# Row sums of a 16384 x 1024 array: another assignment of rows to partitions, line-aligned buffers, and a last row in equal halves

## The chip, the cores and the metric

The kernel runs on one core of a Trainium2 chip. The metric is the device time in microseconds (us); three runs of the kernel before gave a median of 161.55 us.

## The reference

`x` has shape 32 x 512 x 1024 in float32, and the output is `np.sum(x, axis=-1)`, 32 x 512 in float32. Taken flat, there are 16,384 rows of 1,024 numbers (4 KB a row, 67.1 MB in all), and one sum is wanted for each row (64 KB in all).

## The kernel before

The 16,384 rows are spread over the 128 partitions of the on-chip memory, 128 rows for each. They are cut into 8 groups of 2,048 consecutive rows (`x_g`, L120). Within a group, partition p has the 16 rows from 16p on, one run of 64 KB in device memory; the next partition's run follows directly behind it. `rows_from(j, n)` (L123) gives the n rows from the j-th on of every partition. The sums of partition p stand in 128 columns of the tile `sums`, 16 to a group. `out_v` (L121) is the same division of the output, so that a group's sums are 16 consecutive numbers (64 B) for each partition.

Data goes into the tile `t`, of which there are three buffers ("in", bufs=3), each of 16 x 1024 + 4 words in a partition. Every load is issued by SyncE in the helper `rows` (L180). The order is:

1. the first 7 rows of the last group (FIRST = 7). This load is moved to the program's entry, ahead of the start-up barrier;
2. groups 0 to 6, each as one load of 16 rows for every partition (8 MB). From the third buffer on, SyncE may issue a load only when the reduction that read its buffer has ended. Two more waits (`hold`) keep the second load behind a small activation of ScalarE, and the third behind the first reduction;
3. the other 9 rows of the last group, all into one buffer: 6 rows, then 2 rows, then the last row in two pieces, columns 0 to 535 (L231) and 536 to 1023 (L232).

The arithmetic:

- VectorE sums the first 7 rows and groups 0 to 5 with one reduction for each load (`vec`, L141).
- From group 6 on the rows of a load are shared: VectorE takes a row at a time with an add of its two halves that also sums the result (`halves`, L155, each followed by an instruction that reads the sum out), ScalarE takes the others with an activation that accumulates (`act`, L168).
- The last row's first piece is summed to a word that stands right ahead of the second piece (so the second piece is written one word further on); a zero behind the second piece makes the number of words even (L229). The last add then covers that partial sum, the 488 columns and the zero, as two halves of 245 words.

ScalarE's queue stores the sums of groups 0 to 6 (`store`, L191, 7 x 16 columns for each partition), which must wait until the load of 2 rows has landed. SyncE stores the last group's 16 columns after the last add. A hook (`wait_for_the_store_at_the_clear`) has GpSimd wait for that last store at the end of the program.

The seed is one word that VectorE clears (L198) and the small activation reads (L200).

Of the kernel before, what the change touches and what calls it, by code (L numbers as in the profile page):

```python
# [100 lines left out]
@with_exitstack  # L101
def kernel(
    ctx: ExitStack,
    tc: tile.TileContext,
    x: bass.AP,
    out: bass.AP,
):
    nc = tc.nc
    nc.at_finalize(issue_first_load_at_entry)
    nc.at_finalize(order_waits)  # L110
    nc.at_finalize(wait_for_the_store_at_the_clear)
    fp32 = mybir.dt.float32
    P = 128
    batch, seq, dim = x.shape
    rows = batch * seq
    J = rows // P
    BIG = 16


    x_g = x.flatten_outer_dims().rearrange("(g p j) d -> g p j d", p=P, j=BIG)  # L120
    out_v = out.rearrange("b s -> (b s)").rearrange("(g p j) -> p g j", p=P, j=BIG)  # L121

    def rows_from(j, n):  # L123
        return x_g[j // BIG, :, j % BIG : j % BIG + n, :]

    last = J // BIG - 1
    FIRST = 7
    pieces = (536, 488)  # L130

    with (
        tc.tile_pool(name="in", bufs=3) as inpool,
        tc.tile_pool(name="unread", bufs=4, space=bass.MemoryType.PSUM) as upool,
        tc.tile_pool(name="stage", bufs=1) as stpool,
        tc.manual_schedule(),
    ):
        sums = stpool.tile([P, J], fp32)

        def vec(dst, src):  # L140
            return nc.vector.tensor_reduce(  # L141
                out=dst, in_=src, axis=mybir.AxisListType.X, op=mybir.AluOpType.add
            )

        def hold(inst, until, reason):
            tc.add_manual_dep(
                inst.ins,
                until.ins.name,
                mybir.DependencyInfo(mybir.DependencyClass.Sync, mybir.DependencyReason.DATA),
                reason=reason,  # L150
            )

        def halves(dst, src):
            n = src.shape[-1] // 2
            return nc.vector.tensor_tensor_reduce(  # L155
                out=src[:, :n],
                in0=src[:, :n],
                in1=src[:, n:],
                scale=1.0,
                scalar=0.0,  # L160
                op0=mybir.AluOpType.add,
                op1=mybir.AluOpType.add,
                accum_out=dst,
            )

        def act(dst, src, n):
            unread = upool.tile([P, dim], fp32)
            nc.scalar.activation(  # L168
                out=unread[:, :n],
                in_=src,  # L170
                func=mybir.ActivationFunctionType.Copy,
                accum_out=dst,
            )

        sums_of = []

        def rows(t, a, n, j, n_act, pairs=False):
            nv = n - n_act
            block = t[:, a * dim : (a + n) * dim].rearrange("p (n d) -> p n d", d=dim)
            load = nc.sync.dma_start(out=block, in_=rows_from(j, n))  # L180
            if pairs:
                for q in range(nv):
                    sums_of.append(halves(sums[:, j + q : j + q + 1], block[:, q, :]))
            else:
                sums_of.append(vec(sums[:, j : j + nv], block[:, :nv, :]))
            for q in range(nv, n):
                act(sums[:, j + q : j + q + 1], block[:, q, :], dim)
            return load

        def store(eng, g0, g1):  # L190
            return eng.dma_start(  # L191
                out=out_v[:, g0:g1],
                in_=sums[:, g0 * BIG : g1 * BIG].rearrange("p (g j) -> p g j", j=BIG),
            )


        seed = stpool.tile([P, 1], fp32)
        nc.vector.memset(seed, 0.0)  # L198
        unread = upool.tile([P, dim], fp32)
        ready = nc.scalar.activation(  # L200
            out=unread[:, :1], in_=seed, func=mybir.ActivationFunctionType.Copy
        )

        j = last * BIG
        t = inpool.tile([P, BIG * dim + 4], fp32)
        rows(t, 0, FIRST, j, 0)
        first = sums_of[-1]
        for g in range(last):
            t = inpool.tile([P, BIG * dim + 4], fp32)
            if g < last - 1:  # L210
                load = rows(t, 0, BIG, g * BIG, 0)
            else:
                rows(t, 0, BIG, g * BIG, 7, pairs=True)
            if g == 0:
                hold(load, ready, "no second load while the first one's descriptors are made")
            if g == 1:
                hold(load, first, "no descriptors of later loads while the first ones start")

        t = inpool.tile([P, BIG * dim + 4], fp32)
        rows(t, FIRST, 6, j + FIRST, 2, pairs=True)  # L220
        two = rows(t, FIRST + 6, 2, j + FIRST + 6, 1, pairs=True)
        a = BIG - 1

        j += a
        c, width = pieces
        whole = t[:, a * dim + c : BIG * dim + 2]
        nc.vector.memset(whole[:, width + 1 :], 0.0)  # L229
        part = t[:, a * dim : a * dim + c]  # L230
        nc.sync.dma_start(out=part, in_=rows_from(j, 1)[:, 0, :c])  # L231
        nc.sync.dma_start(out=whole[:, 1 : width + 1], in_=rows_from(j, 1)[:, 0, c:])  # L232
        hold(store(nc.scalar, 0, last), two, "its packets come behind those of the loads")
        halves(whole[:, :1], part)
        halves(sums[:, j : j + 1], whole)
        store(nc.sync, last, last + 1)


# [28 lines left out]
```

## Time and profile before

| what | value |
|---|---|
| median of three runs | 161.55 us (161.54 to 162.11) |
| span of the profiled execution | 159.83 us |
| median less that span | 1.72 us |
| VectorE busy | 120.7 us, 76% |
| ScalarE busy | 12.1 us, 8% |
| DMA packets | 2,784, 67.18 MB, mean 420 GB/s |
| reduction of 16 rows | 17.22 us, six times |
| reduction of 7 rows | 7.62 us, once |
| add of 512 words | 0.69 us, 14 times |
| activation of 1,024 words | 1.01 us, ten times |

The profiled execution's own time beside its span is not listed, only those of the three runs; so the table gives the distance from the span to their median. The span runs from SyncE's first issue to the last event that the profile shows. Busy times are shares of that span. An engine's idle time ahead of an instruction is put down to what ended it; a DMA's landing is the time at which its semaphore lets a waiting instruction start. The trace also holds a record of each DMA packet, with its start, its duration and its size; a load or store makes one packet for each run of consecutive bytes, here one for each partition, except the store of seven groups, which has seven for each.

### The profile page before, as it was taken

The numbers are of one execution on the slowest core, as the hardware profiler recorded it, in microseconds if no ns is written. First come the engines' busy times: TensorE is split into PE (matmuls) and PEld (weight loads), VectorE is DVE, ScalarE is ACT, GpSimd is POOL, SyncE is SP. The second block draws the span as 40 slices with busy tenths as digits, with TensorE's granted clock in tenths as the row PEclk, the third lists the DMA queues.
The fourth block names the chain that finished last, engine by engine and source line by source line (L and its number), as shares of the span: only waits on it lengthen the run. The fifth ranks groups of instructions, "written<-read, shape, count | busy, mean of one in ns | idle before, by whom it ended". The sixth has DMA issues, their size and how long they took to land.

```text
span 159.8 us, 134 instructions
## 1 busy us (share of the span) xinstructions
DVE 120.7 (76%) x41; ACT 12.1 (8%) x22; POOL 0.2 (0%) x4
## 2 busy tenths in 40 slices
DVE  0029600399995999779995899949999499994955
ACT  3000000000000000000000000000000000003993
POOL 0000000000000000000000000000000000000000
DMA  8899899699699699699699799898996996996994
GB/s 316 373 492 525 361 426 525 295 492 525 262 525 525 262 525 525 262 525 508 279 525 459 328 525 426 361 525 377 410 525 295 492 525 262 525 525 258 431 382 127
DMA packets 2784, 67.18 MB, mean 420 GB/s; under 512 B 1248, under 2 KB 1376, under 8 KB 1504
## 3 DMA queue, kind: packets, MB, share of 16 engines
q1 hardware_dynamic: 1872, 67.12, 97.7%
q10 hardware_dynamic: 912, 0.06, 0.3%
HBM read 67.11 MB, written 0.07 MB: 420 GB/s over the span
## 4 chain that ended last, share of the span: by engine, by line
DMA 71%; DVE 27%; SPq 1%; issue 0%; DVEq 0%
DMA t<-in_x_dram 71%; DVE sums L141 26%; SPq L180 0%; SPq L231 0%; DVE t L155 0%; DVEq L262 0%
## 5 line engine op out<-in xcount | busy, mean ns | idle before, releaser
L141 DVE TENSOR_REDUCE sums<-t 128x16 f32<-128x16384 f32 (+1 forms) x7 | 110.9, 15849 | 32.5 <-DMA t<-in_x_dram 32.5
L168 ACT ACTIVATE unread<-t 128x1024 f32<-128x1024 f32 x10 | 10.1, 1010 | 144.6 <-DMA t<-in_x_dram 144.6
L155 DVE CUSTOM_DVE_ANT_0 t<-t 128x512 f32<-128x512 f32 (+2 forms) x16 | 9.6, 656 | 4.0 <-DMA t<-in_x_dram 3.9
L168 ACT ACTIVATION_READ_ACCUMULATOR unread<-t 128x1 f32 x10 | 1.9, 186 | 0.0
L200 ACT ACT_TABLE_LOAD x1 | 1.3, 1283 | 0.8 <-PEq L251 0.8
L155 DVE DVE_READ_ACCUMULATOR2_ANT sums<- 128x1 f32 x15 | 1.3, 84 | 0.0
L198 DVE MEMSET seed<- 128x1 f32 x1 | 0.1, 59 | 0.8 <-PEq L251 0.8
L200 ACT ACTIVATE unread<-seed 128x1 f32<-128x1 f32 x1 | 0.2, 174 | 0.0
L251 POOL MEMSET const-bfloat16-1.0<- 128x1 bf16 x1 | 0.1, 101 | 0.0
L251 POOL MEMSET const-uint8-127<- 128x1 uint8 x1 | 0.1, 101 | 0.0
L251 POOL MEMSET const-float32-0.0<- 128x1 f32 x1 | 0.1, 98 | 0.2 <-issue 0.2
L251 POOL MEMSET const-float32-1.0<- 128x1 f32 x1 | 0.1, 98 | 0.0
L155 DVE DVE_READ_ACCUMULATOR2_ANT t<- 128x1 f32 x1 | 0.1, 83 | 0.0
L229 DVE MEMSET t<- 128x1 f32 x1 | 0.1, 59 | 0.0
## 6 DMA issues: line engine op xcount, KB each, us to landing
t<-in_x_dram SPq DMA_DIRECT2D x1, 3584.0 KB, 11.0
t<-in_x_dram SPq DMA_DIRECT2D x1, 3072.0 KB, 28.8
t<-in_x_dram SPq DMA_DIRECT2D x1, 1024.0 KB, 30.9
t<-in_x_dram SPq DMA_DIRECT2D x1, 268.0 KB, 31.1
t<-in_x_dram SPq DMA_DIRECT2D x1, 244.0 KB, 31.2
t<-in_x_dram SPq DMA_DIRECT2D x7, 40.8
out_dram<-sums ACTq DMA_DIRECT2D x1, 56.0 KB, 2.1
out_dram<-sums SPq DMA_DIRECT2D x1, 8.0 KB, 1.4
```

What stands on the lines that cost most here:

```text
L141: return nc.vector.tensor_reduce(out=dst, in_=src, axis=mybir.AxisListType.X, op=mybir.AluOpType.add)
L155: return nc.vector.tensor_tensor_reduce(out=src[:, :n], in0=src[:, :n], in1=src[:, n:], scale=1.0, scalar=0.0, op0=mybir.AluOpType.add, op ...
L168: nc.scalar.activation(out=unread[:, :n], in_=src, func=mybir.ActivationFunctionType.Copy, accum_out=dst,)
L198: nc.vector.memset(seed, 0.0)
L200: ready = nc.scalar.activation(out=unread[:, :1], in_=seed, func=mybir.ActivationFunctionType.Copy)
L229: nc.vector.memset(whole[:, width + 1 :], 0.0)
L251: nc = _bacc.Bacc("TRN2", target_bir_lowering=False, num_devices=1)
```

## The change

- The first 2,048 rows still lie 16 to a partition (`x_a`). The other 14,336 rows lie 112 to a partition (`x_b`): partition p has 112 consecutive rows, a run of 448 KB, and a load of 16 of them takes 64 KB out of each such run. The columns of `sums` 0 to 111 belong to `x_b`, 112 to 127 to `x_a`.
- The order of loads: the 7 rows from the 96th on of each partition in `x_b`; then the 16 rows of `x_a`; then the rows 0 to 95 of `x_b`, 16 at a time; then rows 103 to 111 in loads of 6 and 2 rows and two pieces.
- A buffer has 16 x 1024 + 64 words. The seed moves to a pool of its own ahead of the buffers and takes 32 words; in the built program the buffers then start at multiples of 256 bytes (16,640, 82,432 and 148,224 of a partition; before, 16,512, 82,080 and 147,648).
- The last row comes in pieces of 512 and 512 columns. The first piece's sum goes behind the second piece, which starts at its own place and no longer one word further on. The last add has two halves of 257 words.
- ScalarE's queue stores in two DMAs: the first 96 columns of `x_b` (384 B for each partition), and the 16 of `x_a` (64 B). SyncE's last store has the last 16 columns of `x_b`, 64 B for each partition as before.

```diff
-    x_g = x.flatten_outer_dims().rearrange("(g p j) d -> g p j d", p=P, j=BIG)
-    out_v = out.rearrange("b s -> (b s)").rearrange("(g p j) -> p g j", p=P, j=BIG)
+    LONG = J - BIG
+    rows_in = x.flatten_outer_dims()
+    rows_out = out.rearrange("b s -> (b s)")
+    x_a = rows_in[: P * BIG].rearrange("(p j) d -> p j d", p=P)
+    x_b = rows_in[P * BIG :].rearrange("(p j) d -> p j d", p=P)
+    out_a = rows_out[: P * BIG].rearrange("(p j) -> p j", p=P)
+    out_b = rows_out[P * BIG :].rearrange("(p j) -> p j", p=P)
     def rows_from(j, n):
-        return x_g[j // BIG, :, j % BIG : j % BIG + n, :]
-    last = J // BIG - 1
+        return x_b[:, j : j + n, :] if j < LONG else x_a[:, j - LONG : j - LONG + n, :]
+    last = LONG - BIG
     FIRST = 7
-    pieces = (536, 488)
+    pieces = (512, 512)
+    LINE = 64
...
+        tc.tile_pool(name="small", bufs=1) as smallpool,
...
+        seed = smallpool.tile([P, LINE // 2], fp32)
...
-        def store(eng, g0, g1):
-            return eng.dma_start(
-                out=out_v[:, g0:g1],
-                in_=sums[:, g0 * BIG : g1 * BIG].rearrange("p (g j) -> p g j", j=BIG),
-            )
-        seed = stpool.tile([P, 1], fp32)
+        def store(eng, dst, j0, j1):
+            return eng.dma_start(out=dst, in_=sums[:, j0:j1])
...
-        j = last * BIG
-        t = inpool.tile([P, BIG * dim + 4], fp32)
+        j = last
+        t = inpool.tile([P, BIG * dim + LINE], fp32)
         rows(t, 0, FIRST, j, 0)
...
-        for g in range(last):
-            t = inpool.tile([P, BIG * dim + 4], fp32)
-            if g < last - 1:
-                load = rows(t, 0, BIG, g * BIG, 0)
+        wholes = [LONG, *range(0, last, BIG)]
+        for k, at in enumerate(wholes):
+            t = inpool.tile([P, BIG * dim + LINE], fp32)
+            if k < len(wholes) - 1:
+                load = rows(t, 0, BIG, at, 0)
...
-        nc.sync.dma_start(out=whole[:, 1 : width + 1], in_=rows_from(j, 1)[:, 0, c:])
-        hold(store(nc.scalar, 0, last), two, "its packets come behind those of the loads")
-        halves(whole[:, :1], part)
+        nc.sync.dma_start(out=whole[:, :width], in_=rows_from(j, 1)[:, 0, c:])
+        late = "its packets come behind those of the loads"
+        hold(store(nc.scalar, out_b[:, :last], 0, last), two, late)
+        hold(store(nc.scalar, out_a, LONG, J), two, late)
+        halves(whole[:, width : width + 1], part)
         halves(sums[:, j : j + 1], whole)
-        store(nc.sync, last, last + 1)
+        store(nc.sync, out_b[:, last:], last, LONG)
```

## The prediction

> **What bounds the kernel now.** I read the page first (share by engine, DMA queues, chain), then the timeline, then the SyncE queue's waits, and last the single DMA packets of the trace. All times but the final ones are from the profiled execution, whose span is 159.83 us; the median of the three runs is 161.55, so 1.72 us lie outside the span, and I carry them over unchanged.
>
> From the page, the queues (packets, MB, share of 16 engines' span) and the chain by engine:
>
> ```profile
> q1 hardware_dynamic: 1872, 67.12, 97.7%
> q10 hardware_dynamic: 912, 0.06, 0.3%
> HBM read 67.11 MB, written 0.07 MB: 420 GB/s over the span
> ...
> DMA 71%; DVE 27%; SPq 1%; issue 0%; DVEq 0%
> ```
>
> The 16 DMA engines are busy 97.7% of the span with loads alone, VectorE 76%. The 27% of VectorE in the chain could mislead: it stands there because SyncE may issue a load only when the reduction before has freed one of three buffers. The timeline shows that this isn't what sets the pace (start, duration, engine, line; the bracket is the idle time ahead):
>
> ```profile
> 49.73 17.22 DVE L141 TENSOR_REDUCE sums<-t 128x16 f32<-128x16384 f32 x1 [2.13 <-DMA t<-in_x_dram]
> 69.08 17.22 DVE L141 TENSOR_REDUCE sums<-t 128x16 f32<-128x16384 f32 x1 [2.13 <-DMA t<-in_x_dram]
> 88.44 17.22 DVE L141 TENSOR_REDUCE sums<-t 128x16 f32<-128x16384 f32 x1 [2.14 <-DMA t<-in_x_dram]
> 107.78 17.22 DVE L141 TENSOR_REDUCE sums<-t 128x16 f32<-128x16384 f32 x1 [2.13 <-DMA t<-in_x_dram]
> ```
>
> Each reduction of 17.22 us waits 2.13 us for data, and they start 19.35 us apart. The packet records say why. Each DMA makes one packet per partition, 8 for each of 16 engines, and the next load's packets begin on an engine when the last one's end. Median durations by size, beside a straight line drawn through the two largest (0.036784 ns a byte and 7.3 ns a packet):
>
> ```
> bytes  packets  median ns  line ns  where it is written (of load)
> 65536      896       2418     2418  the seven 16-row loads
> 28672      128       1062     1062  the first load, 7 rows
> 24576      128        912      911  6 rows
>  8192      128        309      309  2 rows
>  2144      128         87       86  last row, columns 0 to 535
>  1952      128         80       79  last row, columns 536 to 1023
> ```
>
> Eight packets of 2418 ns and a semaphore write of 9 are 19.35 us, the whole period. So the loads run back to back from the first landing to the last: the span is start-up (first load's last packet ends at 10.68), then 7 x 19.353 + 7.305 + 2.481 + 0.705 + 0.649 = 146.6 us of packets (the records give 146.53, to 157.21), then a tail of 2.6 us. How near is the buffer wait to being the bound? A reduction ends 17.22 us after 69.08, at 86.30; SyncE's issue takes 0.33, and packets follow an issue by about 0.5 (the last store's issue ends at 158.45, its first packet starts at 158.94): 87.15. The first engine needs work at 87.49. About 0.35 us are left in each round.
>
> The tail, from the timeline:
>
> ```profile
> 156.33 0.69 DVE L155 CUSTOM_DVE_ANT_0 t<-t 128x512 f32<-128x512 f32 x1
> 156.42 0.41 ACTq L191 DMA_DIRECT2D out_dram<-sums  x1
> ...
> 157.06 0.44 DVE L155 CUSTOM_DVE_ANT_0 t<-t 128x268 f32<-128x268 f32 x1
> ...
> 157.65 0.42 DVE L155 CUSTOM_DVE_ANT_0 t<-t 128x245 f32<-128x245 f32 x1
> 157.99 0.08 DVE L155 DVE_READ_ACCUMULATOR2_ANT sums<- 128x1 f32 x1
> 158.10 0.35 SPq L191 DMA_DIRECT2D out_dram<-sums  x1
> ```
>
> The last piece lands (packets to 157.21, seen at 157.57), one add of 0.42, the read of its sum, SyncE's store.
>
> **The change, part by part.**
>
> *Instructions.* The changed kernel's program holds the same instructions in the same order on every engine, but for one more DMA issue on ScalarE's queue and the widths of the last two adds. Loads, waits and buffers (three) correspond one for one. So what can move is how long packets take, and the tail.
>
> *Rows laid out 112 to a partition.* Each packet of a 16-row load is 64 KB in one run, as before; but neighbouring partitions' runs now lie 448 KB apart (112 x 4 KB) and no longer 64 KB, except in the load of the 2048 rows. The bytes and the number of packets (56 large ones per engine) stay. The trace of before has no such spacing. Lower bound: the large packets' mean is 2422.6 and their median 2418, so if all unevenness went, 56 x 4.6 ns = 0.26 us would be gained. Upper bound: the nearest uneven row is the seventh 16-row load, in which single packets took up to 2587 ns; it ended 19.49 us after its predecessor where the five intervals before are 19.32 to 19.36. If six loads with the new spacing lost the same 0.15, that is +0.9. I take 0: 434 GB/s is reached in every steady window, the fixed byte cost is the same for 2 KB and 64 KB packets, and a straight line through all sizes leaves no room for a cost that depends on where a run begins.
>
> ```profile
> 69.08:88.44 19.36, 17.22 (x2) 0.00 (x0) 0.00 (x0) 1.00 1.00 433
> 88.44:107.78 19.34, 17.21 (x1) 0.00 (x0) 0.00 (x0) 1.00 1.00 434
> ```
>
> (Columns: window, length, busy time of VectorE, ScalarE and GpSimd with counts, clock, DMA share, GB/s.)
>
> The Trainium skill speaks against this part: "DMA: Bandwidth & Descriptors", section "Latency and other measured facts", reports copies at a row pitch of 512 KiB at 207 GB/s where padded pitches reach 214, and far less at 2 to 8 MiB. Its 3.3% on 146.5 us would be 4.8 us, an estimate by the Trainium skill; no run here shows it yet, and 448 KB is no power of two.
>
> *First load.* Its first packets are slow (1152 to 1918 ns against 1062) whatever they read; with other addresses I expect the same. Bounds: nothing gained, and one more packet per engine as slow as the first, some +0.6 us.
>
> *Buffers that start on whole lines of 256 B* (16,388 to 16,448 words each, and the seed moved ahead of them). Bounds: no gain; or all of the 7.3 ns that each packet costs beside its bytes, on 12 loads x 8 = 96 packets per engine, 0.70 us. The row nearest to the question is the last piece: its destination starts one word past the first piece's end and its source 2144 bytes into a row, the worst placed packets of the kernel. They lie 0.9 ns above the line, those of the first piece 0.8. Bad placement costs at most about a nanosecond a packet there, so I take half of that: 96 x 0.5 = -0.05 us.
>
> The Trainium skill ("DMA: Bandwidth & Descriptors", section "How a descriptor splits into AXI transactions") says that a start off a 256 B boundary fetches unused bytes and costs beats. By it the last piece's packets, 96 B past a boundary, would carry three spare beats, together 3.5 ns at its 850 MHz; the trace disagrees, with 0.1 ns between the two pieces.
>
> *Last row as 512 and 512.* The packets of 2048 B come to 82.7 ns by the line, 16 of them per engine 1.32 us against 8 x 87 + 8 x 80 = 1.34: the second piece lands at the same time, within 0.02. The first add (256 in place of 268) shrinks, and waits for nothing but the row before; the last one, which is on the path, grows from 245 to 257 elements: (437 - 417) / 23 = 0.87 ns an element, +0.01 us.
>
> *Stores.* 896 packets of 64 B become 128 of 384 and 128 of 64. They ran from 157.37 to 158.10, after the last load packet (157.21) and before the last store's first (158.94): on nobody's way, so fewer of them gain nothing. The extra issue on ScalarE's queue takes 0.41 after 156.83, to 157.24; behind it is only the end of the program, which SyncE reaches after 158.45. Covered by 1.2 us; uncovered it would be +0.41. The last store is as before, 16 columns of 64 B, at +1.4 us.
>
> *Sum:* 0 + 0 - 0.05 + 0.01 + 0 = -0.04 us: 161.55 becomes 161.5.
>
> **The rivals.**
>
> *Placement pays after all:* each packet sheds its 7.3 ns, -0.70 us, 160.85; with the unevenness gone too, 160.6. For it: those 7.3 ns are in every packet, and the three buffers now start at bytes 16,512, 82,080 and 147,648 of a partition in the built program, none a multiple of 256. Against it: the worst placed packets cost no more than the others. The pace of VectorE would not stop it: 58 ns a round is far below the 0.35 us that are left.
>
> *Wide spacing slows the reads* (the one that ends slower). The place is the 16-row loads with 448 KB between runs, the price what the seventh load lost per round, six times 0.15 = +0.9, 162.45; with a second slow packet in the first load +1.5, 163.0. It decides if a large packet's mean passes 2437 ns (0.81 us over 56 packets is 14.5 ns each above today's mean of 2422.6); an engine also falls idle if the spread of the 16 engines' ends, 0.53 us now, grows beyond 0.9, since SyncE's next issue is only 0.35 us early. For it: the one uneven load shows that large packets can be slowed at random. Against: 16 streams of whole 64 KB runs, all sizes on one line. The pitch rule of the Trainium skill named above would make it 166, which is outside the range.
>
> *The extra issue or its completion delays the end:* +0.41, 161.95. It needs ScalarE to be last, and it is 1.2 us early.
>
> **How the numbers follow.** No change of note (161.2 to 161.9): 0.66. Placement pays: 0.14, half of it near 160.85 and half below 160.74. Spacing slows: 0.15, most of it above 162.36. Late end: 0.05. About 0.5% (0.81 us) is what a measurement of this kernel can tell from no change; the runs of before alone spread over 0.57. So faster by more 0.07, slower by more 0.13, within 0.80. The range takes in the full placement gain (160.85) and the spacing's first price (162.45) with a little beside them: 160.8 to 162.6.
>
> **What would show it.** In the changed kernel's packets: large ones at 2418 (2411 if placement pays, a mean above 2437 if spacing hurts); reductions 19.35 us apart, idle 2.13 before each; 2048 B packets near 83 ns; 288 packets on the store queue, ended before 158.2; the last add 0.43 long and the last issue near 158.1. The forecast is wrong if the starts of the reductions drift from 19.35 apart, or if the last issue moves against the last landing.

## The result and the profile after

The changed kernel takes 161.21 us in the median of 13 runs (161.12 to 161.27), the kernel before 161.55 (161.45 to 162.11, 13 runs). The ratio is 0.9971, with a 95% interval of 0.9963 to 0.9979: a real gain of some 0.3%, less than the 0.5% that the prediction set as its bound, and more than the 0.04 us that it expected. Beside the experiments the changed kernel was run again, with 161.23 and a ratio of 0.9979 (0.9970 to 0.9987).

The page of the changed kernel, queues and chain:

```profile
q1 hardware_dynamic: 1872, 67.12, 97.8%
q10 hardware_dynamic: 288, 0.06, 0.2%
HBM read 67.11 MB, written 0.07 MB: 421 GB/s over the span
...
DMA 71%; DVE 27%; SPq 1%; issue 0%; DVEq 0%
```

The bound is what it was: the loads' queue is busy 97.8% of the span. Only the store queue's packets fell, from 912 to 288. The timeline of the changed kernel (start, duration, engine, line, and in brackets the idle time ahead):

```profile
10.79 7.62 DVE L152 TENSOR_REDUCE sums<-t 128x7 f32<-128x7168 f32 x1 [9.89 <-DMA t<-in_x_dram]
30.13 17.22 DVE L152 TENSOR_REDUCE sums<-t 128x16 f32<-128x16384 f32 x1 [11.72 <-DMA t<-in_x_dram]
49.53 17.22 DVE L152 TENSOR_REDUCE sums<-t 128x16 f32<-128x16384 f32 x1 [2.17 <-DMA t<-in_x_dram]
68.88 17.22 DVE L152 TENSOR_REDUCE sums<-t 128x16 f32<-128x16384 f32 x1 [2.13 <-DMA t<-in_x_dram]
...
157.25 0.43 DVE L166 CUSTOM_DVE_ANT_0 t<-t 128x257 f32<-128x257 f32 x1 [0.21 <-DMA t<-in_x_dram]
157.60 0.08 DVE L166 DVE_READ_ACCUMULATOR2_ANT sums<- 128x1 f32 x1
157.71 0.35 SPq L202 DMA_DIRECT2D out_dram<-sums  x1
```

The first reduction starts 0.26 us earlier than before (10.79 against 11.05), and the last issue 0.39 us earlier (157.71 against 158.10). The span is 159.44 against 159.83, and this execution's own time is 161.23. By the packets, 0.23 of the 0.39 are there when the first load ends (last packet at 10.45 against 10.68). The rest comes from two places. The seven 16-row loads together took 135.42 us of packets in place of 135.52: the seventh 19.34 and not 19.49, most of the others a little longer. (A round is here the time from the last packet of one load to the last packet of the next.) And the last add starts 0.37 us after the last load packet, where it started 0.43 after it. Of these 0.43 only 0.36 are the way from the packet (157.21) to the landing; for 0.08 more the chain of the kernel before shows no wait:

```profile
126.38 31.19 DMA t<-in_x_dram
157.57 0.08 issue
157.65 0.42 DVE t L155
```

In the changed kernel the landing comes 0.34 us after the packet. So these two profiles alone show no shorter way of the last piece; the experiments do. To see such differences I took from the packet records three numbers for each kernel: when the first load's last packet ends, how many of its third to sixth packets per engine (64 in all, in order of start) took over 1080 ns, and the lag, the time from a load's last packet to the start of the instruction that reads it.

```
                  rows apart  buffers  first load  slow of  lag in us of   median (lowest to
kernel            (KB)        mod 256  ends, us    64       g0     last    highest) us
before            64          off      10.68       16       0.36   0.43    161.55 (161.45-162.11)
after             448         0        10.45       1        0.33   0.37    161.21 (161.12-161.27)
e1_aligned        64          0        10.68       15       0.35   0.38    161.48 (161.32-162.32)
e2_halves         64          off      10.70       20       0.36   0.47    161.68 (161.54-161.92)
e3_layout         448         off      10.49       0        0.35   0.46    161.46 (161.34-161.74)
e4_store_runs     64          off      10.71       15       0.36   0.47    161.85 (161.52-162.08)
e5_pieces_back    448         0        10.57       0        0.33   0.38    161.28 (161.16-161.43)
e6_ends_dense     64 / 448    0        10.68       12       0.34   0.32    161.34 (161.30-161.46)
e7_pitch512       512         0        11.01       1        0.33   0.31    161.81 (161.70-162.16)
e8_off_line       448         160      10.70       0        0.36   0.46    161.44 (161.34-161.70)
e9_odd_pitch      452         0        10.63       1        0.38   0.35    161.50 (161.30-161.72)
e10_line64        448         192      10.43       0        0.37   0.49    161.38 (161.32-161.67)
e11_old_rows      64          0        10.58       13       0.33   0.32    161.53 (161.25-161.87)
e12_again         448         0        10.41       0        0.33   0.32    161.23 (161.11-161.40)
```

"Rows apart" is the distance of neighbouring partitions' runs in the first load (and, where they differ, in most 16-row loads); "off" means that the three buffers start 128, 160 and 192 bytes past a multiple of 256. "g0" is the first 16-row load, "last" the last piece. The columns from the first load's end to the lag are of one execution each, the medians are of 11 to 13 runs. The kernel before had medians of 161.55 (beside e1 to e4), 161.62 (e5 to e8) and 161.51 (e9 to e12).

### The profile page after: what moved, and what is told of

The parts are those of the page before. It is cut to its first block, busy times and chain, and to the rows that moved or that the text cites. A ratio compares the mean times of both kernels' runs of the same rounds, so it can differ in the third digit from the quotient of the medians.

```text
span 159.4 us, 135 instructions
## 1 busy us (share of the span) xinstructions
DVE 120.6 (76%) x41; ACT 12.1 (8%) x22; POOL 0.2 (0%) x4
## 3 DMA queue, kind: packets, MB, share of 16 engines
q1 hardware_dynamic: 1872, 67.12, 97.8%
## 4 chain that ended last, share of the span: by engine, by line
DMA 71%; DVE 27%; SPq 1%; issue 0%; DVEq 0%
DMA t<-in_x_dram 71%; DVE sums L152 26%; SPq L191 0%; SPq L236 0%; DVE t L166 0%; DVEq L269 0%
```

## The experiments

### One part at a time

My first theory was A, that aligned buffers make packets cheaper. Its rivals were B, the rows' places; C, VectorE's chain in the tail; and D, fewer store packets.

**e1_aligned**, buffers alone:

```diff
+        tc.tile_pool(name="small", bufs=1) as smallpool,
         tc.tile_pool(name="in", bufs=3) as inpool,
...
+        seed = smallpool.tile([P, LINE // 2], fp32)
...
-        t = inpool.tile([P, BIG * dim + 4], fp32)
+        t = inpool.tile([P, BIG * dim + LINE], fp32)
```

> One part of the change alone: buffers that start at multiples of 256 bytes (64 spare words, seed ahead of them); rows, stores and the last row's pieces as before. Theory A (line starts make packets cheaper): the whole -0.34 us of the change is here, about 161.2, and the large packets' median falls below 2418 ns or the first load ends 0.2 us earlier. Theory B (the rows' new places in device memory do it): 161.55, no difference. Theory C (the tail's VectorE chain does it): 161.55. Theory D (fewer store packets): 161.55.

161.48, ratio 1.0001 (0.9988 to 1.0014). A failed as stated: the packets' median stayed at 2418 ns, the first load ended at 10.68, and the time didn't fall clear of the noise. But the last add started 0.38 us after the last packet, as in the changed kernel.

**e2_halves**, the last row's pieces alone:

```diff
-    pieces = (536, 488)
+    pieces = (512, 512)
-        nc.sync.dma_start(out=whole[:, 1 : width + 1], in_=rows_from(j, 1)[:, 0, c:])
+        nc.sync.dma_start(out=whole[:, :width], in_=rows_from(j, 1)[:, 0, c:])
-        halves(whole[:, :1], part)
+        halves(whole[:, width : width + 1], part)
```

> One part alone: the last row as 512 and 512 columns, the second piece at its own place and the partial sum behind it. Theory C: the last add in the kernel before starts 0.08 us after its data since VectorE is only just ready, and the earlier first piece cures that; about 0.07 us faster, 161.48, last add within 0.03 of the landing. Theories A, B and D: 161.55, within 0.05; the added 12 words of the last add would cost 0.01.

161.68, ratio 1.0003 (0.9993 to 1.0013). C is out: VectorE was ready 0.19 us ahead of the last piece in this kernel's profile, and still the lag was 0.47 and nothing was gained. Its profiled execution (161.81) had three uneven rounds, 19.44, 19.49 and 19.39 us, with packets of up to 2602 ns.

**e3_layout**, rows and stores alone (`x_a`, `x_b` and the two early stores of the change; buffers, seed and pieces of before):

> One part alone: 2048 rows 16 to a partition and 14336 rows 112 to a partition, with the stores in two DMAs that this brings; buffers and the last row's pieces as before. Theory B: the -0.34 us is here, 161.2, first load ended earlier by 0.2 us. Theory A: 161.55. Theory D (fewer store packets, 256 in place of 896, at the end): also faster, but the gain stands behind the last load's landing, not ahead of it. Spacing that hurts: 161.7 or more, with an aligned sibling that makes up for it.

161.46, ratio 0.9990 (0.9980 to 1.0000). About a quarter of the change's gain by the medians; the first load ended at 10.49, so B had a part right, but the lag was still 0.46.

**e4_store_runs**, the early store as one run for each partition:

```diff
-        hold(store(nc.scalar, 0, last), two, "its packets come behind those of the loads")
+        flat = out.rearrange("b s -> (b s)")[: P * last * BIG].rearrange("(p j) -> p j", p=P)
+        early = nc.scalar.dma_start(out=flat, in_=sums[:, : last * BIG])
+        hold(early, two, "its packets come behind those of the loads")
```

> Stores alone: the kernel before, but ScalarE's store writes a partition's 112 sums as one run of 448 bytes (128 packets in place of 896), so the sums stand in other places of the output than the reference's; loads and sums as before. Theory D: up to 0.3 us faster, 161.25 to 161.45, with the gain behind the last landing. Theories A, B and C: 161.55, within 0.05, since the 896 packets ran when no load was left.

161.85, ratio 1.0010 (1.0001 to 1.0020). Fewer store packets give nothing; D is out.

No part alone gave the gain. The table suggested a new theory: two sources, the alignment through the lag and the rows through the first load, whose gains must be seen together and against the changed kernel.

### One part undone

**e5_pieces_back** is the changed kernel with the pieces of before (the reverse of e2's diff).

> The changed kernel with the last row again as 536 and 488 columns, the second piece one word off. Theory now: the gain has two sources, the first load (rows 448 KB apart, 0.23 us earlier) and the lag from last packet to reader (aligned buffers, 0.37 in place of 0.43 to 0.47 us); the pieces give nothing: 161.2, within 0.05 of the changed kernel, last add within 0.38 of the last packet. Rival (the second piece's own placement makes the lag): 161.3, lag 0.44 or more.

161.28, ratio 0.9977 (0.9968 to 0.9986): the gain is still there. The last piece's own placement, one word off, doesn't make a lag of 0.44 or more (0.38 here; e1 and e5, the two with aligned buffers and this piece, have the longest of the eight aligned kernels). Against the changed kernel's 161.21 and 161.23, measured at other times, 0.05 to 0.07 is left that these runs don't resolve.

**e8_off_line** moves the changed kernel's three buffers and nothing else:

```diff
-        seed = smallpool.tile([P, LINE // 2], fp32)
+        seed = smallpool.tile([P, 8], fp32)
```

> The changed kernel with all three buffers moved to 160 bytes past a multiple of 256 (seed of 8 words in place of 32), nothing else. If aligned buffers shorten the lag: lag of the last reads 0.44 or more, growing over the loads, time 161.3 or more. If the alignment is idle: 161.2 and lags of 0.33 to 0.38 as in the changed kernel.

161.44, ratio 0.9989 (0.9980 to 0.9998): 0.2 us of the gain are lost (0.16 against e5, which was measured beside it). The lags rise from load to load, 0.36, 0.37, 0.39, 0.42, 0.44, 0.46 and 0.47 for the seven 16-row loads, 0.47 and 0.49 for the next two, while the packets take 2418 ns as ever. In the tail of this kernel:

```profile
157.37 0.08 DVE L166 DVE_READ_ACCUMULATOR2_ANT t<- 128x1 f32 x1
157.63 0.43 DVE L166 CUSTOM_DVE_ANT_0 t<-t 128x257 f32<-128x257 f32 x1 [0.18 <-DMA t<-in_x_dram]
157.98 0.08 DVE L166 DVE_READ_ACCUMULATOR2_ANT sums<- 128x1 f32 x1
158.09 0.35 SPq L202 DMA_DIRECT2D out_dram<-sums  x1
```

VectorE is idle for 0.18 us ahead of the last add, so the landing sets it. The last packet ended at 157.17, and the add starts at 157.63. (This execution took 161.61, more than its kernel's median; its first load ended late, at 10.70.)

**e10_line64** puts them on multiples of 64 bytes (`smallpool.tile([P, 16], fp32)`):

> The changed kernel with its buffers 192 bytes past multiples of 256: on multiples of 64 bytes, no longer on multiples of 256. If 64 bytes are enough: 161.2, lag of the last reads 0.33 to 0.38. If it takes 256: as with 160 bytes past, 161.44, the lag growing to 0.46.

161.38, ratio 0.9989 (0.9980 to 0.9998), 0.15 above the changed kernel measured beside it (e12 below). The lag grows from 0.37 to 0.49. 64 bytes are not enough. The last add of this kernel, and below it that of e12, whose last packets end at 156.90 and 156.88:

```profile
157.38 0.43 DVE L166 CUSTOM_DVE_ANT_0 t<-t 128x257 f32<-128x257 f32 x1 [0.20 <-DMA t<-in_x_dram]
157.19 0.43 DVE L166 CUSTOM_DVE_ANT_0 t<-t 128x257 f32<-128x257 f32 x1 [0.19 <-DMA t<-in_x_dram]
```

VectorE waits for the landing in both, and it comes 0.17 us later here.

**e6_ends_dense** exchanges the two kinds of rows:

```diff
-    last = LONG - BIG
+    last = LONG
-        wholes = [LONG, *range(0, last, BIG)]
+        wholes = [*range(0, LONG, BIG)]
-        hold(store(nc.scalar, out_b[:, :last], 0, last), two, late)
-        hold(store(nc.scalar, out_a, LONG, J), two, late)
+        hold(store(nc.scalar, out_b, 0, LONG), two, late)
-        store(nc.sync, out_b[:, last:], last, LONG)
+        store(nc.sync, out_a, LONG, J)
```

> The changed kernel with the two kinds of rows exchanged: the first load and the end come from the 2048 rows that lie 16 to a partition (64 KB apart), all seven 16-row loads from the rows 112 to a partition. If the spacing in the first load alone gives its part: first load ends at 10.68 again and the time is 161.42. If it is what the following loads read that matters (seven in place of six with wide spacing): 161.2 and first load at 10.45. Seven wide loads also cost 0.01 more than six if the 19.34 against 19.33 us a round of the traces is the spacing.

161.34, ratio 0.9982 (0.9974 to 0.9991), between the two expectations. The first load ended at 10.68 again and 0.11 to 0.13 us are lost, not 0.21 (0.06 against e5, which was measured beside it). Wide spacing in the 16-row loads costs nothing (rounds of 19.32 to 19.34), and the runs stay within 0.16 us of each other.

**e11_old_rows** is the changed kernel with the rows and stores of before (e1's and e2's diffs together):

> The changed kernel with the rows and stores of before: aligned buffers and equal pieces stay, all groups lie 16 rows to a partition again. Theory of two sources: the alignment's share is kept and the rows' share is lost, 161.40 to 161.50, first load ended near 10.68, lags 0.33 to 0.38, and single runs up to 0.8 above the median, which the changed kernel doesn't show. Rival (alignment alone with equal pieces gives all): 161.2.

161.53, ratio 0.9998 (0.9987 to 1.0009), where I expected 161.40 to 161.50; the changed kernel measured beside it had 161.23. So without the new rows all of the gain is gone in the median, though the lag (0.32) is as short as in e12. The runs suggest how: they reach from 161.25 to 161.87, and the profiled one, 161.27, had even rounds. Old rows leave a kernel whose good runs are near the changed kernel's and whose others are not. Its lowest run is also 0.14 below the lowest of 35 runs of the kernel before at that time (161.39), so the shorter lag may show there.

**e12_again**, the changed kernel:

> The changed kernel itself once more beside the other three: 161.2, runs within 0.15 of each other. Its first load's end tells whether 10.45 was chance: 10.40 to 10.57 if it goes with the rows 448 KB apart, 10.68 if it doesn't.

161.23. First load at 10.41, no slow packet, all runs within 0.29 of each other (0.15 expected).

### Other spacings

**e7_pitch512**, one run of 128 rows for each partition:

```diff
-    LONG = J - BIG
+    LONG = J
-    x_b = rows_in[P * BIG :].rearrange("(p j) d -> p j d", p=P)
+    x_b = rows_in.rearrange("(p j) d -> p j d", p=P)
-        wholes = [LONG, *range(0, last, BIG)]
+        wholes = [*range(0, last, BIG)]
```

> The changed kernel with all 16384 rows laid 128 to a partition, neighbouring partitions' runs 512 KB apart, a power of two. If any wide spacing does what 448 KB does: first load ends near 10.45, rounds of 19.34, 161.2. If the Trainium skill's rule for row pitches that are powers of two holds here (DMA: Bandwidth & Descriptors, Latency and other measured facts: 207 against 214 GB/s at 512 KiB): rounds of 19.9 or more and 165 to 166. By the traces alone: between 161.1 and 163, since one uneven round cost 0.15.

161.81, ratio 1.0016 (1.0007 to 1.0025): 0.6 us slower than the changed kernel (0.5 against e5, measured beside it). The time of 165 to 166 that the expectation works out from the Trainium skill ("DMA: Bandwidth & Descriptors", section "Latency and other measured facts") did not come. The timeline of this kernel:

```profile
11.38 7.62 DVE L150 TENSOR_REDUCE sums<-t 128x7 f32<-128x7168 f32 x1 [10.48 <-DMA t<-in_x_dram]
30.68 17.22 DVE L150 TENSOR_REDUCE sums<-t 128x16 f32<-128x16384 f32 x1 [11.68 <-DMA t<-in_x_dram]
50.01 17.22 DVE L150 TENSOR_REDUCE sums<-t 128x16 f32<-128x16384 f32 x1 [2.11 <-DMA t<-in_x_dram]
69.41 17.22 DVE L150 TENSOR_REDUCE sums<-t 128x16 f32<-128x16384 f32 x1 [2.17 <-DMA t<-in_x_dram]
```

The loss is all there at the first landing, 11.38 against 10.79; from then on the reductions start 19.3 to 19.4 us apart as in the changed kernel. All 11 runs are at 161.70 or above, so the loss is not of the profiled run alone. In the first load the engines' first packets start from 0.99 to 2.14 us (in the changed kernel from 0.99 to 1.97, in its second profile to 1.78, in the kernel before to 1.67).

**e9_odd_pitch**, 113 rows and 15 (452 KB apart), the row left over loaded by itself:

```diff
-    LONG = J - BIG
+    LONG = J - BIG + 1
+    SHORT = J - LONG
-            load = nc.sync.dma_start(out=block, in_=rows_from(j, n))
+            if j == LONG - 1:
+                load = nc.sync.dma_start(out=block[:, :1, :], in_=rows_from(j, 1))
+                nc.sync.dma_start(out=block[:, 1:, :], in_=rows_from(LONG, SHORT))
+            else:
+                load = nc.sync.dma_start(out=block, in_=rows_from(j, n))
```

> The changed kernel with 113 rows to a partition in place of 112 (an odd number, runs 452 KB apart) and 15 in place of 16; the one row left over is loaded beside the 15 in a load of its own, and the early stores become three. If the start of the first load is slow because runs lie at multiples of 64 KB: its packets after the first two are all 1062 ns and it ends before 10.40; less the extra load's 8 packets per engine at some 8 ns, 0.06 us, the time is 161.0 to 161.15. If any wide spacing is as good: 161.27, the extra packets alone. Rounds stay near 19.34.

161.50, ratio 0.9998 (0.9989 to 1.0006): worse than either expectation. The slow packets were gone (1 of 64), but the first load ended at 10.63, and the runs spread over 0.4 us. Multiples of 64 KB are not what hurts: 448 and 512 KB are such multiples too and have 0 or 1 slow packets.

## Why the prediction was right, and where it was wrong

The forecast was 161.5 in a range of 160.8 to 162.6, and no change beyond 0.5%; 161.21 is inside both. The range was that wide for the rivals' prices, so lying in it says little for the sum. A sum of -0.04 us where -0.34 is measured has steps that failed.

- **Instructions, bound, buffer wait: right.** The loads run back to back in every kernel, reductions idle 2.1 us each round, and SyncE's margin was never used up.
- **Buffers on whole lines: mis-sized.** The step took -0.05 us, from the rule that the worst placed packets last no longer than the others. For the large packets that holds: with the changed kernel's buffers and with e8's they take the same 2418 ns. But how long a packet is recorded isn't all that alignment can move.

  In the four kernels with buffers off a multiple of 256 and even rounds (e3, e4, e8 and e10) the lag from last packet to reader grows from 0.35 to 0.37 us at the first 16-row load to 0.46 to 0.49 at the last piece; in e2 and the kernel before, whose rounds were uneven, it rises and falls back, and ends at 0.47 and 0.43. With aligned buffers it ends at 0.31 to 0.38, in all eight. The landings of the 16 engines, paired with the ends of their packets in order of time, agree: the median distance rises from 0.35 to 0.46 us in e10 (first 16-row load to 2-row load) and stays between 0.31 and 0.35 in e12. That is 0.1 to 0.17 us, and in e8 and e10 the 6-row and 2-row packets were longer too (means of 913.5 and 312 ns against 912 and 309). By the medians it is worth 0.15 (e10 against e12, measured together) to 0.2 (e8), with the new rows; with the old ones the medians show at most 0.07 of it (e1). The rival "placement pays" had the part right and the mechanism wrong: no packet shed its 7.3 ns.
- **A reading of that lag, not shown in itself.** It looks like writes that fall behind the reads by a little at each packet: from the first 16-row load to the last piece e10's lag grows by 0.12 us over 80 packets per engine, 1.5 ns each. In the kernel before it rose to 0.43 by the fifth 16-row load, and was back at 0.37 after the seventh, the one whose reads were uneven, which may have given the writes time. The records show no writes apart from reads, so this stays an inference. The Trainium skill ("DMA: Bandwidth & Descriptors", section "How a descriptor splits into AXI transactions") says for starts off a 256 B boundary that the bytes below the start are fetched and cost beats. It speaks of what is read and not of where it is written, so it bears on this by likeness alone. That 256 and not 64 bytes decide is like e10. The size is not: by the Trainium skill's 32 B a beat and 850 MHz the 192 spare bytes of e10 would be six beats, an estimate of 7 ns, where e10 shows 1.5.
- **Rows 448 KB apart: taken as 0, and a gain.** The prediction took 0 for the wide spacing, since "a straight line through all sizes leaves no room" for a cost of where a run begins, and saw in it a loss sooner than a gain. In fact it removes the slow packets of the first load, 12 to 20 of 64 in each of the six kernels with 64 KB between runs and 0 or 1 in each of the eight others. The step on the first load, "with other addresses I expect the same", failed there: it ended at 10.41 to 10.57 in five of the six profiles with 448 KB, and at 10.58 to 10.71 in all six with 64. The slow packets are only part of such a difference. Over 1062 ns each they cost an engine 0.06 to 0.10 us on average in the six kernels. The rest lies in the first two packets of each engine, which end at the latest between 4.06 and 4.35 us (4.66 at 512 KB) with either distance: e8 has no slow packet, but the last of its second packets ended at 4.35, and its first load at 10.70.
- **Its worth.** With aligned buffers the new rows are worth 0.3 us in the median (e11 against e12, measured together). e6 splits it, across runs of different times: wide 16-row loads 161.53 to 161.34, a wide first load 161.34 to 161.21 or 161.23 (or 161.28, e5, measured beside e6). For the first load the slow packets account for 0.06 to 0.10, as above. For the 16-row loads the profiles show less. Single runs of e1, e11 and the kernel before lie 0.6 to 1.0 us above the lowest of their kernel. Two profiled executions with old rows, of the kernel before and of e2 (161.81), had rounds of 19.39 to 19.49 us; the other three, of e1, e4 and e11, had none, but they were among the shortest of their kernels (161.39, 161.55, 161.27). None of the profiles with 448 KB has a round above 19.36. That uneven rounds make the spread is likely, and rests on two executions.
- **Unevenness as a term: right in kind.** The step kept 0.26 us as the lower bound, if all of it went; the large packets' mean fell from 2422.6 to 2420.1 ns, and 56 x 2.5 ns are 0.14.
- **Stores, pieces, extra issue: right.** e4 and e5 show no gain from the first two beyond 0.07 us; the second issue of ScalarE ended at 156.99, 0.7 us ahead of SyncE's last.
- **The slower rival.** It did not happen at 448 KB. At 512 KB it did, with 0.5 to 0.6 us, but in the first load and not in the rounds where I had put it.

The two parts do not add up one by one: alone they measure -0.07 and -0.09, together -0.28 to -0.34. A kernel whose rounds are now and then uneven may hide 0.1 us, which no run here shows by itself, and off-line buffers spread the runs of the new rows too (e3, e8 and e10: 0.35 to 0.40 us, against 0.15 and 0.29 for the changed kernel).

What stays open: why the kernel with 452 KB, which has 1 slow packet, takes 0.27 us more in the median than the one with 448 measured beside it and spreads more (it also has a load and a store more, and its one profile ended the first load 0.2 us later); why at 512 KB several engines' first packets start so late; and what makes a round uneven.

## What to carry to other kernels

When a kernel is bound by its loads, look at how the loads land, not only at how long their packets take: read the lag from last packet to first reader, load by load, and see whether it grows. Small parts of a change should be tested by undoing each in the changed kernel as well as by doing each alone in the old one, and by their spread as well as their medians; here neither part showed its worth alone. Start buffers that a DMA fills on multiples of 256 bytes (here worth 0.15 to 0.2 of 161 us; multiples of 128 were not tried by themselves), and try several distances between the partitions' rows for the first load, which starts on all engines at once.

## What the runs showed of the hardware that was not expected

Alignment of the destination left the recorded length of the large packets as it was (a median of 2418 ns for 64 KB in every kernel), yet it moved the last landing by 0.1 to 0.17 us, and starts at multiples of 64 bytes (e10) did as badly as starts 32 past one (e8). A distance of 512 KB between runs left the steady rate alone: rounds of 19.34 us are 434 GB/s. The Trainium skill ("DMA: Bandwidth & Descriptors", section "Latency and other measured facts") reports 3% less at that pitch for copies between tensors in HBM; for loads to the on-chip memory e7's rounds don't show it. Only its first load was late (11.01 us), and whether that has to do with the pitch's being a power of two is open.
